# A two-layer hybrid trunk on one core: the logarithm by a polynomial, one more load buffer, and 108 shifted priorities

## The chip, the cores and the metric

The kernel runs on one core of a Trainium2 chip. The metric is the device time of one execution in microseconds; the median of three runs of the kernel before is 618.05 us (617.97 to 618.89). The core's engines work side by side, each through its own queue of instructions: TensorE (PE in the profile, and PEld for its weight loads), VectorE (DVE), ScalarE (ACT), GpSimd (POOL) and SyncE (SP, which here only issues DMAs). They wait for each other at semaphores.

## The reference, cut to what matters

Two layers over 256 tokens of width 1024, in float32. A layer normalises its input, sends it through one combined projection `w_in` (1024 x 9808), runs three causal attention mixers of eight 64-wide heads on parts of the result, gates each, projects each with its `w_branch`, adds the three under per-channel gates, and sends the sum through `w_out` onto the residual. The third mixer adds a running sum of log-sigmoids to its logits, and this is where the logarithm is:

```python
proj = jnp.einsum('bsd,de->bse', rms_norm(x, gain), w_in)
...
# mixer b: the 64 keys with the largest index score, per query
rel = jax.nn.relu(jnp.einsum('bqhd,bsd->bqhs', qi, k_idx))
isc = jnp.einsum('bqh,bqhs->bqs', wi, rel)
ival, idx = lax.top_k(isc, top)
...
# mixer c: forgetting attention
log_f = jax.nn.log_sigmoid(f_logit + f_bias)          # 256 tokens x 8 heads
csum = jnp.cumsum(log_f, axis=1)
s = q @ k.T * scale + (cq[..., :, None] - csum[:, :, None, :])
...
merged = sum(sigmoid(merge_logit) * y for the three branches)
x = x + merged @ w_out
```

## The kernel before

All weights stream once from HBM through a ring of 1 MB buffers, `raw` (three of them, `R_RAW = 3`). To keep float32 accuracy on TensorE each weight is split in two parts, a rounded high part `wh` and the rest `wl`, and each product is three matmuls: high by high, high by low, low by high. ACT writes `wh` (a copy of 128 x 1024, L374), DVE subtracts it from `raw` to give `wl` (L378), and PE reads both. Each has a ring of six buffers.

PE's work comes in *units*. A unit of kind B computes 128 columns of a projection for all 256 tokens: 24 matmuls of 128 x 256 into one PSUM bank `proj`. A unit of kind A has 128 tokens and 512 columns; a unit Y belongs to `w_branch`. Between the units stand the small groups of the attention: the scores of a pair of heads (six matmuls into the banks `s`, of which there are two, L604 and L606), the transposes of the probabilities (three per head into a bank `t`, L692), and the product with the values (eight matmuls into the only bank `o`, L708 to L711).

A layer runs: norm and transpose of the input, the values of mixer a, the small unit `kwf` (index key, index weights, forget logits), four units of the index query `qi` with their scores, then the mixers a, c and b with the units of the merge gates and of `w_branch` between them, then `w_out`. What this text calls the *index stage* is the stretch from `kwf` to the first attention of mixer a, 30 to 90 us in layer 0 and 330 to 390 us in layer 1. There, ACT takes the ReLU of the index scores out of the two `s` banks (L818 and L819), DVE adds them up over heads into `isc` (L827, L829) and then finds the 64 largest of each row in eight rounds of MAX8 and MATCH_REPLACE8 (L849, L850). Rotary embedding goes through DVE and POOL: a shuffle into `rsh` and a product into `rr` on DVE (L468, L470), a product and a sum on POOL (L469, L471). Of `rsh` and `rr` there are two buffers each.

In the index stage also stands the logarithm, in `wf_cols`, on tiles of 128 x 16 called `fz`: with z the logit, e = exp(-|z|) and u = ln(1 + e) on ACT (L777, L778), then nine small DVE instructions (L782 to L790) that correct u for small e and end in min(z, 0) - u. Two matmuls on PE (L796, L797) then make the running sum, `csum`. The function ln is in another activation table than the others, so ACT loads a table ahead of ln and another ahead of the next tanh (L863).

No order is written out by hand. The program records its operations one after the other, each with its engine (or engines), an estimated cost, what it reads and writes, and a *key*, mostly the number of its unit plus an offset. `Plan.run` then lays them out: it takes the engine that can start something earliest, and on it, of the operations that could start by then, the one with the smallest key. The instructions are issued in that order, and each engine's queue keeps it.

```python
lim = best[e] + slack.get(e, 0.0)
t, _, _, o, w = min((c for c in cand if c[4][0] == e and c[0] <= lim), key=lambda c: (c[1], c[2]))
```

Of the kernel before, what the change touches and what calls it, by code (L numbers as in the profile page):

```python
# [9 lines left out]
F32 = mybir.dt.float32  # L10
F32R = mybir.dt.float32r
AF = mybir.ActivationFunctionType
ALU = mybir.AluOpType
# [14 lines left out]
NR = {"a": 0, "b": 1, "c": 2}  # L28

C_ID, C_UT, C_MASK, C_ROPE, C_END = 0, 128, 256, 512, 1024  # L30
SWAP = list(range(8, 16)) + list(range(0, 8)) + list(range(16, 32))

R_RING = 6
R_RAW = 3
TAIL = {"ACT": 95.0, "DVE": 85.0, "POOL": 0.0, "PE": 0.0, "SP": 0.0}
STEP = 24.0
SPLIT_LEAD = 2.0
# [14 lines left out]
def shape_constants():  # L52
    c = np.zeros((128, C_END), np.float32)
    i = np.arange(128)
    c[:, C_ID:C_ID + 128] = np.eye(128)
    c[:, C_UT:C_UT + 128] = i[:, None] <= i[None, :]
    diag = np.where(i[None, :] <= i[:, None], 0.0, MASKED)
    c[:, C_MASK + 128:C_MASK + 256] = diag
    inv = np.power(np.float32(500000.0), -np.arange(0, 16, 2, dtype=np.float32) / np.float32(16))
    ang = np.arange(S, dtype=np.float32)[None, :] * inv.astype(np.float32)[:, None]  # L60
    cos, sin = np.cos(ang).astype(np.float32), np.sin(ang).astype(np.float32)
    ct = np.ones((128, S), np.float32)
    st = np.zeros((128, S), np.float32)
    for b in (0, 64):
        ct[b:b + 8] = cos
        ct[b + 8:b + 16] = cos
        st[b:b + 8] = -sin
        st[b + 8:b + 16] = sin
    c[:, C_ROPE:C_ROPE + 256] = ct
    c[:, C_ROPE + 256:C_ROPE + 512] = st  # L70
    return c


CUR = [""]
# [21 lines left out]
class Plan:  # L96
# [8 lines left out]
    def op(self, ways, reads, writes, key, lag=0.0, name="", touch=()):  # L105
        o = Op()
        o.ways, o.key, o.lag, o.name, o.margin, o.port, o.half = ways, key, lag, name, 0.0, False, False
        deps, o.bufs = {}, []
        for t in reads:
            for d in t.w:  # L110
                deps[id(d)] = d
        for t in writes:
            for d in t.w + t.r:
                deps[id(d)] = d
        for t in reads:
            t.r.append(o)
        for t in writes:
            t.w, t.r = [o], []
        for t in {id(t): t for t in list(reads) + list(writes) + list(touch)}.values():
            if isinstance(t, Buf):  # L120
                if t.no is None:
                    t.no = self.made[t.tag] = self.made.get(t.tag, -1) + 1
                t.left += 1
                o.bufs.append(t)
        o.deps = list(deps.values())
        o.n, o.out, o.need, o.end = len(self.ops), [], 0, None
        for d in o.deps:
            if d is not o:
                d.out.append(o)
                o.need += 1  # L130
        self.ops.append(o)
        return o
# [111 lines left out]
def hybrid_trunk(ctx, tc, x, norm_gain, w_in, forget_bias, w_branch, w_out, final_gain, consts, out):  # L244
# [97 lines left out]
    plan.tag("pth", pts[:1])  # L342
    plan.tag("ptl", pts[1:])
    plan.tag("bd", bd)
    for nm, n, cols, dt in (("rsh", 2, S, F32), ("rr", 2, S, F32),
                            ("th", 2, S, F32), ("g", 4, S, F32), ("e", 4, 384, F32), ("st", 8, 8, F32),
                            ("fb", 2, 384, F32), ("ot", 2, S, F32), ("t8", 4, 8, F32), ("mth", MTH, S, F32)):
        tag(nm, n, [128, cols], dt)
# [409 lines left out]
    def wf_cols(l, key):  # L758
        ps = Buf("t")

        def tr():
            for t in range(2):
                PE.transpose(T(ps)[:, t * 16:t * 16 + 16], wf[64:80, t * 128:(t + 1) * 128], ident[64:80, 64:80])
        pe(tr, 220.0, [k_wf, k_id], [ps], key, "wf")
        v = lambda: T(ps)[:, :32].rearrange("p (t c) -> p t c", t=2)
        sc = float(np.float32(8 ** -0.5 * 64 ** -0.5))
        dve(lambda: DVE.tensor_scalar(widx, v()[:, :, 0:8], sc, None, op0=ALU.mult), 16, [ps], [k_widx], key, "wf")
        z, na, e, u, c, lf = [fz[:, i].rearrange("p (t c) -> p t c", t=2) for i in range(6)]
        fb = fbias[:, l:l + 1, :].to_broadcast([128, 2, 8])

        def pre():
            DVE.tensor_tensor(z, v()[:, :, 8:16], fb, op=ALU.add)
            DVE.scalar_tensor_tensor(na, z, -1.0, z, op0=ALU.mult, op1=ALU.min)
        dve(pre, 0, [ps, k_fb], [k_lf], key, "lf", 300.0)

        def ln():
            ACT.activation(e, na, AF.Exp)  # L777
            ACT.activation(u, e, AF.Ln, bias=1.0)  # L778
        act(ln, 0, False, [], [k_lf], key, "ln", 1540.0)
        act(lambda: None, 0, False, [k_lf], [], key - 1, "table", 1190.0)  # L780

        for f in (lambda: DVE.tensor_scalar(c, e, 1.0, None, op0=ALU.add),  # L782
                  lambda: DVE.tensor_scalar(na, c, 1.0, None, op0=ALU.is_equal),
                  lambda: DVE.tensor_scalar(c, c, -1.0, 5e-8, op0=ALU.add, op1=ALU.max),
                  lambda: DVE.reciprocal(c, c),
                  lambda: DVE.tensor_tensor(c, c, e, op=ALU.mult),
                  lambda: DVE.tensor_tensor(u, u, c, op=ALU.mult),
                  lambda: DVE.tensor_tensor(na, na, e, op=ALU.mult),
                  lambda: DVE.tensor_tensor(u, u, na, op=ALU.add),
                  lambda: DVE.scalar_tensor_tensor(lf, z, 0.0, u, op0=ALU.min, op1=ALU.subtract)):  # L790
            dve(f, 0, [], [k_lf], key + 10, "lf", 100.0, port=True)

        cs = Buf("t")

        def cum():
            PE.matmul(T(cs)[:, :16], ut, lf.rearrange("p t c -> p (t c)"), start=True, stop=False)  # L796
            PE.matmul(T(cs)[:, 8:16], ones, lf[:, 0], start=False, stop=True)  # L797
        pe(cum, 400.0, [k_lf, k_cst], [cs], key + 10, "csum", MARGIN)
        w = lambda: T(cs)[:, :16].rearrange("p (t c) -> p t c", t=2)
        dve(lambda: DVE.tensor_copy(csum, w()), 16, [cs], [k_cs], key, "csum")  # L800
        dve(lambda: DVE.tensor_scalar(ncs, w(), -1.0, None, op0=ALU.mult), 16, [cs], [k_cs], key, "csum")
        rep, k_rep = wf.rearrange("p (t r c) -> p t r c", t=2, r=16), Tok()
        dve(lambda: DVE.tensor_copy(rep, w().unsqueeze(2).to_broadcast([128, 2, 16, 8])), S, [cs], [k_rep, k_wf], key + 10, "csum")
        pt = Buf("t")

        def tr2():
            for t in range(2):
                PE.transpose(T(pt)[:, t * 128:(t + 1) * 128], wf[:, t * 128:(t + 1) * 128], ident)
        pe(tr2, 225.0, [k_rep, k_id], [pt], key + 10, "cT", MARGIN)
        act(lambda: ACT.activation(cT, T(pt)[:, :S], AF.Copy), S, True, [pt], [k_rep, k_cT], key + 10, "cT")  # L810
# [306 lines left out]
```

## Time and profile before

| | |
|---|---|
| runs, median (range) | 618.05 us (617.97 to 618.89) |
| the profiled execution's own time | 618.74 us |
| its span, first to last instruction | 616.9 us |
| PE busy | 606.5 us, 4804 matmuls |
| PEld busy | 581.1 us |
| DVE busy | 534.5 us |
| ACT busy | 451.7 us |
| POOL busy | 95.0 us |
| granted TensorE clock, mean | 0.997 |
| moved by DMA | 107.32 MB, 174 GB/s |

The profile page gives busy times of engines, a chain of work that ended last, and groups of instructions. The trace behind it can be asked for the instructions in order of time and for who waited for whom. Matmuls are pipelined, so two that follow each other overlap in the trace, and "PE busy" is not a measure of PE at its peak; from one start to the next is. A number in brackets at a row's end, such as `[0.37 <-ACT tmp L819]`, is the idle time of the engine just before it and what ended it.

### The profile page before, as it was taken

What the parts mean: (1) busy time and instruction counts of PE and PEld (TensorE: products, weight loads), DVE (VectorE), ACT (ScalarE), POOL (GpSimd) and SP (SyncE); (2) the same over time, 40 slices, a digit from 0 to 9 for tenths busy, and PEclk for the clock granted to TensorE, in tenths of its full rate; (3) what the DMA queues carried; (4) which work ended last, traced back from release to release, by engine and by line L of the source; (5) the groups of instructions that cost most, each with busy time, mean ns of one, the idle gap of its engine ahead of it and who ended that gap; (6) DMA issues with size and microseconds to landing.
All of it is one profiled execution on the core that took longest, in us unless ns stands there. A gap on an engine that the chain in (4) does not pass through costs nothing.

```text
span 616.9 us, 12615 instructions
## 1 busy us (share of the span) xinstructions
PE 606.5 (98%) x4804; PEld 581.1 (94%) x4804; DVE 534.5 (87%) x1322; ACT 451.7 (73%) x948; POOL 95.0 (15%) x101
## 2 busy tenths in 40 slices
PE   8999999999999999999999999999999999999995
PEld 6899999999998999999889999998999989999985
DVE  7899999985998889988588999998678988999773
ACT  5788398876996778775587866997688766987541
POOL 1251242000000233200006305300000013220001
PEclk9999999999999999999999999999999999999998
DMA  8962765655554563575555639455637365453711
GB/s 283 304 195 90 226 171 191 200 171 172 171 173 136 180 197 99 175 237 173 158 170 174 204 114 276 141 170 185 209 103 231 112 201 157 155 169 122 257 35 69
DMA packets 96156, 107.32 MB, mean 174 GB/s; under 512 B 4576, under 2 KB 84832, under 8 KB 96096
## 3 DMA queue, kind: packets, MB, share of 16 engines
q1 hardware_dynamic: 95808, 106.13, 54.7%
q8 instruction: 37, 0.61, 0.4%
q10 hardware_dynamic: 288, 0.39, 0.2%
q14 instruction: 23, 0.19, 0.1%
HBM read 103.37 MB, written 1.05 MB: 169 GB/s over the span
## 4 chain that ended last, share of the span: by engine, by line
PE 78%; DVE 13%; ACT 4%; issue 2%; DMA 1%; POOL 1%; SPq 0%; POOLq 0%; DVEq 0%; ACTq 0%
PE proj L419 68%; DVE wl L378 5%; PE t L692 3%; DVE isc L850 2%; PE proj L996 1%; PE s L604 1%; PE s L606 1%; DVE t L849 1%; DMA x<-in_x_dram 1%; DVE isc L829 1%; DVE rsh L468 1%; ACT wh L374 1%; PE o L708 1%; PE o L711 1%; DVE rr L470 1%
## 5 line engine op out<-in xcount | busy, mean ns | idle before, releaser
L419 PE MATMUL proj<-hTh,wh 128*128 128x256 f32 (+1 forms) x1040 | 270.1, 278 | 0.0
L419 PE MATMUL proj<-hTl,wh 128*128 128x256 f32 (+1 forms) x1040 | 269.7, 277 | 0.0
L378 DVE TENSOR_TENSOR wl<-raw,wh 128x1024 fp32r<-128x1024 f32 (+1 forms) x190 | 235.5, 1248 | 38.3 <-ACT wh L374 37.7
L374 ACT ACTIVATE wh<-raw 128x1024 fp32r<-128x1024 f32 (+1 forms) x190 | 199.0, 1053 | 51.1 <-PE proj L419 41.3
L419 PE MATMUL proj<-hTh,wl 128*128 128x256 f32 (+1 forms) x1040 | 234.0, 278 | 0.0
L419 PEld LDWEIGHTS proj<-hTh,wh 128*128 128x128 f32 (+1 forms) x1040 | 194.7, 187 | 0.2
L419 PEld LDWEIGHTS proj<-hTl,wh 128*128 128x128 f32 (+1 forms) x1040 | 194.6, 187 | 0.3
L419 PEld LDWEIGHTS proj<-hTh,wl 128*128 128x128 f32 (+1 forms) x1040 | 175.6, 187 | 0.0
L469 POOL TENSOR_TENSOR rsh<-rsh,cst 128x256 f32<-128x256 f32 (+1 forms) x42 | 35.6, 849 | 351.9 <-DVE rsh L468 351.7
L471 POOL TENSOR_TENSOR rr<-rr,rsh 128x256 f32<-128x256 f32 (+1 forms) x42 | 51.1, 1220 | 8.2 <-DVE rr L470 5.4
L669 ACT ACTIVATE e<-e,st 128x128 f32<-128x128 f32 x96 | 42.7, 446 | 6.9 <-DVE st L665 6.6
L419 PE MATMUL proj<-wh,v 128*128 128x512 f32 (+1 forms) x144 | 35.5, 368 | 0.0
L419 PE MATMUL proj<-og0l,wh 128*128 128x256 f32 x128 | 33.9, 277 | 0.0
L419 PE MATMUL proj<-og0h,wh 128*128 128x256 f32 x128 | 32.4, 278 | 0.0
L419 PE MATMUL proj<-wh,hTh 128*128 128x512 f32 x80 | 32.4, 405 | 0.0
L419 PE MATMUL proj<-wh,hTl 128*128 128x512 f32 x80 | 31.5, 393 | 0.0
L419 PEld LDWEIGHTS proj<-wh,v 128*128 128x128 f32 x144 | 25.2, 188 | 4.7
L419 PE MATMUL proj<-og0h,wl 128*128 128x256 f32 x128 | 28.6, 277 | 0.0
L697 DVE TENSOR_TENSOR ptl<-t,pth 128x384 fp32r<-128x384 f32 x48 | 24.9, 551 | 0.6 <-ACT pth L695 0.6
L419 PE MATMUL proj<-wl,hTh 128*128 128x512 f32 x80 | 24.9, 392 | 0.0
L419 PEld LDWEIGHTS proj<-og0h,wh 128*128 128x128 f32 x128 | 24.0, 188 | 0.0
L419 PEld LDWEIGHTS proj<-og0l,wh 128*128 128x128 f32 x128 | 24.0, 188 | 0.0
(194 smaller groups left out, 1046.1 us busy)
## 6 DMA issues: line engine op xcount, KB each, us to landing
raw<-in_w_in_dram SPq DMA_DIRECT2D x74, 1024.0 KB, 5.3
raw<-in_w_branch_dram SPq DMA_DIRECT2D x24, 512.0 KB, 3.5
raw<-in_w_out_dram SPq DMA_DIRECT2D x8, 1024.0 KB, 6.9
tmp<-wf SPq DMA_DIRECT2D x16, 128.0 KB, 5.2
raw<-in_w_in_dram SPq DMA_DIRECT2D x3, 512.0 KB, 7.9
x<-in_x_dram SPq DMA_DIRECT2D x4, 256.0 KB, 5.1
raw<-in_w_in_dram SPq DMA_DIRECT2D x2, 320.0 KB, 6.0
out_dram<-tmp SPq DMA_DIRECT2D x2, 320.0 KB, 2.5
```

The costliest lines, as they stand in the source:

```text
L374: ACT.activation(p[0].v, sel(c.v), AF.Copy)
L378: DVE.tensor_tensor(p[1].v, sel(c.v), p[0].v.bitcast(F32), op=ALU.subtract)
L419: PE.matmul(o(), a(), b(), start=first and i == 0, stop=last and i == n - 1)
L468: dve(lambda: DVE.stream_shuffle(T(sh)[:np_], a(), SWAP), S, [ps], [sh], key, "rope")
L469: gps(lambda: POOL.tensor_tensor(T(sh)[:np_], T(sh)[:np_], s[:np_], op=ALU.mult), S, [k_rope], [sh], key, "rope")
L470: dve(lambda: DVE.tensor_tensor(T(r)[:np_], a(), c[:np_], op=ALU.mult), S, [ps, k_rope], [r], key, "rope")
L471: gps(lambda: POOL.tensor_tensor(T(r)[:np_], T(r)[:np_], T(sh)[:np_], op=ALU.add), S, [sh], [r], key, "rope")
L604: PE.matmul(o.rearrange("p (h c) -> p h c", h=2), qh[:, sl], kl[:, :, :n], start=True, stop=False)
L669: act(lambda t=t, a=a, n=n, e=e, st=st: ACT.activation(T(e)[:, a:a + n], T(e)[:, a:a + n], AF.Exp, bias=T(st)[:, t:t + 1], scale=-1.0, acc ...
L692: PE.transpose(T(ps)[:, i * 128:(i + 1) * 128], T(es[h])[:, i * 128:(i + 1) * 128], ident)
L697: dve(lambda h=h, src=src: DVE.tensor_tensor(T(pl)[:, h], src(), T(ph)[:, h].bitcast(F32), op=ALU.subtract), 384, [ps, kp[h][0]], [kp[h][1 ...
L850: dve(lambda o=o, t8=t8: DVE.match_replace(o, T(t8), o, TAKEN), n, [t8], [k_isc[i]], key + r * step, "top8")
```

## The change

Five edits go together.

1. The logarithm. ln(1 + e) is computed as 2 atanh(s) with s = e / (e + 2), as an odd polynomial in s with five coefficients. ACT keeps the exponential and loses the logarithm and the two table loads; DVE has ten small instructions in the place of nine.
2. `R_RAW` goes from 3 to 4: four load buffers.
3. `rsh` and `rr` go from two buffers each to four.
4. A table `SHIFT` adds a number between -10 and +2 to the keys of 108 operations, by their place in the recording (the last one in the table is operation 2954).
5. `dynamic_dma_scratch_size=1024` is given to the program's constructor, which leaves SBUF for the new buffers.

Below the table every line of the file stands 14 to 16 lines further down: L374 becomes L390, L378 becomes L394, L692 becomes L708, and so on.

```diff
+ATANH = (2.0, 0.666663146821, 0.400249102795, 0.279606027472, 0.281783350867)
-R_RAW = 3
+R_RAW = 4
...
+SHIFT = {
+    142: -3, 143: -4, 145: -4, 192: -3, 231: -1, 233: -4, 264: -2, 349: -3, 350: 2, 391: 1, 396: -1, 398: -4,
...
+        o.key += SHIFT.get(o.n, 0.0)
...
-    for nm, n, cols, dt in (("rsh", 2, S, F32), ("rr", 2, S, F32),
+    for nm, n, cols, dt in (("rsh", 4, S, F32), ("rr", 4, S, F32),
...
-        def ln():
-            ACT.activation(e, na, AF.Exp)
-            ACT.activation(u, e, AF.Ln, bias=1.0)
-        act(ln, 0, False, [], [k_lf], key, "ln", 1540.0)
-        act(lambda: None, 0, False, [k_lf], [], key - 1, "table", 1190.0)
-
-        for f in (lambda: DVE.tensor_scalar(c, e, 1.0, None, op0=ALU.add),
-                  lambda: DVE.tensor_scalar(na, c, 1.0, None, op0=ALU.is_equal),
-                  lambda: DVE.tensor_scalar(c, c, -1.0, 5e-8, op0=ALU.add, op1=ALU.max),
-                  lambda: DVE.reciprocal(c, c),
-                  lambda: DVE.tensor_tensor(c, c, e, op=ALU.mult),
-                  lambda: DVE.tensor_tensor(u, u, c, op=ALU.mult),
-                  lambda: DVE.tensor_tensor(na, na, e, op=ALU.mult),
-                  lambda: DVE.tensor_tensor(u, u, na, op=ALU.add),
-                  lambda: DVE.scalar_tensor_tensor(lf, z, 0.0, u, op0=ALU.min, op1=ALU.subtract)):
+        act(lambda: ACT.activation(e, na, AF.Exp), 16, False, [], [k_lf], key, "lf")
+
+        s, s2, q = na, c, u
+        for f in (lambda: DVE.tensor_scalar(s2, e, 2.0, None, op0=ALU.add),
+                  lambda: DVE.reciprocal(s2, s2),
+                  lambda: DVE.tensor_tensor(s, e, s2, op=ALU.mult),
+                  lambda: DVE.tensor_tensor(s2, s, s, op=ALU.mult),
+                  lambda: DVE.tensor_scalar(q, s2, ATANH[4], ATANH[3], op0=ALU.mult, op1=ALU.add),
+                  lambda: DVE.tensor_tensor(q, q, s2, op=ALU.mult),
+                  lambda: DVE.scalar_tensor_tensor(q, q, ATANH[2], s2, op0=ALU.add, op1=ALU.mult),
+                  lambda: DVE.scalar_tensor_tensor(q, q, ATANH[1], s2, op0=ALU.add, op1=ALU.mult),
+                  lambda: DVE.scalar_tensor_tensor(q, q, ATANH[0], s, op0=ALU.add, op1=ALU.mult),
+                  lambda: DVE.scalar_tensor_tensor(lf, z, 0.0, q, op0=ALU.min, op1=ALU.subtract)):
...
-    nc = _bacc.Bacc("TRN2", target_bir_lowering=False, num_devices=1)
+    nc = _bacc.Bacc("TRN2", target_bir_lowering=False, num_devices=1, dynamic_dma_scratch_size=1024)
```

What the five edits do to the order is seen at three places. The number and the shapes of PE's matmuls are the same in both programs. In the rows below, a name is a tile and the number behind it says which buffer.

The first place is ACT's queue in the index stage of layer 0, between the ReLU of the second index pair (`tmp_108<-s`) and that of the third. The `q` names are the three forms of an index query that PE reads. Before:

```order
L819 ACTIVATE tmp_108<-s_163 128x512
L591 ACTIVATE qy_87<-qh_81 64x256
L591 ACTIVATE qx_85<-qh_82 64x256
L591 ACTIVATE qx_85<-qy_88 64x256
L591 ACTIVATE qx_83<-qh_80 64x256
L591 ACTIVATE qy_88<-qh_82 64x256
L591 ACTIVATE qx_83<-qy_86 64x256
L863 ACTIVATE acc<-proj_161 128x256
L374 ACTIVATE wh_67<-raw_120 128x1024
L818 ACTIVATE tmp_108<-s_162 128x256
L591 ACTIVATE qy_86<-qh_80 64x256
L819 ACTIVATE tmp_108<-s_163 128x512
```

And in the changed program:

```order
L833 ACTIVATE tmp_108<-s_168 128x512
L877 ACTIVATE acc<-proj_166 128x256
L390 ACTIVATE wh_67<-raw_118 128x1024
L607 ACTIVATE qx_83<-qh_80 64x256
L607 ACTIVATE qy_88<-qh_82 64x256
L832 ACTIVATE tmp_108<-s_167 128x256
L607 ACTIVATE qx_83<-qy_86 64x256
L833 ACTIVATE tmp_108<-s_168 128x512
```

Of the eight instructions that stood between the first ReLU shown and the next one, four remain; four of the copies have moved ahead of the first ReLU.

The second place is PE's queue in layer 1, where the running sum of the logarithm (`fz`) is multiplied in the middle of a unit. Before:

```order
L419 MATMUL proj_161<-hTl,wh_68 128x256
L796 MATMUL t_164<-fz,cst 128x16
L797 MATMUL t_164<-fz,ones 128x8
L419 MATMUL proj_161<-hTh,wl_75 128x256
L419 MATMUL proj_161<-hTh,wh_68 128x256
```

And in the changed program:

```order
L435 MATMUL proj_166<-hTh,wl_75 128x256 x2
L435 MATMUL proj_166<-hTh,wh_68 128x256
L435 MATMUL proj_166<-hTl,wh_68 128x256
L810 MATMUL t_170<-fz,cst 128x16
L811 MATMUL t_170<-fz,ones 128x8
L435 MATMUL proj_166<-hTh,wl_75 128x256
```

It is the same unit of B; the two products have moved 12 matmuls further back in it. In layer 0 they have moved 36 further back.

The third place is DVE's queue in layer 1 at the first pair of mixer a. `ISA e,st<-s` adds the mask to the scores and takes the row's extreme; the reciprocal and the product on `e` follow after ACT's exponential, and PE waits for them with its transposes. Before:

```order
L378 TENSOR_TENSOR wl_74<-raw_118,wh_67 128x1024
L665 ISA e_131,st_135<-s_162,cst 128x128
...
L665 ISA e_132,st_136<-s_163,cst 128x256
L665 ISA st_136 128x1
L673 RECIPROCAL st_135<-st_135 128x1
L378 TENSOR_TENSOR wl_75<-raw_118,wh_68 128x1024
L673 RECIPROCAL st_136<-st_136 128x1
L853 TENSOR_SCALAR selb<-isc 128x128
L680 TENSOR_SCALAR e_132<-e_132,st_136 128x128
```

And in the changed program:

```order
L394 TENSOR_TENSOR wl_74<-raw_119,wh_67 128x1024
L394 TENSOR_TENSOR wl_75<-raw_119,wh_68 128x1024
L681 ISA e_136,st_140<-s_167,cst 128x128
...
L681 ISA e_137,st_141<-s_168,cst 128x256
L681 ISA st_141 128x1
L689 RECIPROCAL st_140<-st_140 128x1
L426 SCALAR_TENSOR_TENSOR qy_88<-rr_129,qh_82 128x256
L696 TENSOR_SCALAR e_136<-e_136,st_140 128x128
L689 RECIPROCAL st_140<-st_140 128x1
```

The weight split `wl_75` stood between the scores and the products of the pair, and stands ahead of the scores now. On PE the two heads' transposes of this pair stood 12 matmuls apart, the first of them right behind the next pair's scores; now both stand together, six matmuls behind those scores.

More of the change, by code (lines that the diff above doesn't have):

```diff
@@ L71, in shape_constants @@
     return c
+SHIFT = {
[10 rows of a table added]
+}
 CUR = [""]
```

9 rows, old and new, of the table SHIFT are left out of this document.

## The prediction

> **What bounds the kernel now.** I read the engines' busy times first, then who waited on PE and on its weight loads, then PE's own rows at the places named there, then ACT's and DVE's rows ahead of them.
>
> ```profile
> span 616.9 us, 12615 instructions
> ...
> PE 606.5 (98%) x4804; PEld 581.1 (94%) x4804; DVE 534.5 (87%) x1322; ACT 451.7 (73%) x948; POOL 95.0 (15%) x101
> ```
>
> PE is at work nearly all the time, so an edit on another engine pays only where PE waits. These are all the waits of the weight loads, which come to a semaphore ahead of their matmuls:
>
> ```profile
> PEld proj L996 <- ACT hTh L527: 1.5, 1, 1.5
> PEld proj L996 <- issue: 1.1, 1, 1.1
> PEld t L911 <- DVE ones L907: 1.1, 1, 1.1
> PEld s L604 <- ACT tmp L819: 1.0, 3, 0.5
> PEld t L796 <- DVE fz L790: 0.8, 2, 0.6
> PEld t L520 <- ACT tmp L501: 0.6, 2, 0.4
> PEld proj L996 <- DVE wl L988: 0.6, 1, 0.6
> PEld t L692 <- ACT e L677: 0.3, 1, 0.3
> PEld o L708 <- ACT bd0h L744: 0.3, 1, 0.3
> PEld s L604 <- DVE st L665: 0.2, 1, 0.2
> ```
>
> Lines 911, 996 and 520 are the program's start (and the same transposes at the layer's change), which the order leaves as it is. What is left is 1.0 + 0.8 + 0.3 + 0.3 + 0.2 = 2.6 us: three scores of the index stage that wait for ACT's ReLU, two running sums that wait for the logarithm's last DVE instruction, and three groups of mixer a's first pairs. No unit waits for `wl` or `wh` after the start. So the kernel is bound by PE's own pace, and the change can win little over 2.6 us, or lose.
>
> A wait costs PE more than its idle time, since the matmuls behind it start more slowly. From the first row of a score to the unit's next row, undisturbed and then at the three waits:
>
> ```profile
> 44.56 0.28 PE L604 MATMUL s<-bd0l,qh 128*128 128x256 f32 x1
> ...
> 45.38 0.28 PE L419 MATMUL proj<-hTh,wh 128*128 128x256 f32 x1
> ...
> 48.14 0.38 PE L604 MATMUL s<-bd0l,qh 128*128 128x256 f32 x1
> ...
> 49.06 0.50 PE L604 MATMUL s<-bd0l,qh 128*128 128x512 f32 x1 [0.37 <-ACT tmp L819]
> ...
> 49.64 0.28 PE L419 MATMUL proj<-hTh,wh 128*128 128x256 f32 x1
> ...
> 340.62 0.28 PE L604 MATMUL s<-bd1l,qh 128*128 128x256 f32 x1
> ...
> 341.70 0.28 PE L419 MATMUL proj<-hTh,wh 128*128 128x256 f32 x1
> ...
> 345.13 0.28 PE L604 MATMUL s<-bd1l,qh 128*128 128x256 f32 x1
> ...
> 346.45 0.28 PE L419 MATMUL proj<-hTh,wl 128*128 128x256 f32 x1
> ```
>
> The undisturbed group takes 45.38 - 44.56 = 0.82 us; the others take 1.50, 1.08 and 1.32. The excess is 0.68 + 0.26 + 0.50 = 1.44 us, where the list has 1.0.
>
> **The change part by part.**
>
> *The logarithm.* Per layer ACT loses two table loads and one small instruction; its rows here:
>
> ```profile
> 28.54 0.20 ACT L777 ACTIVATE fz<-fz 128x16 f32<-128x16 f32 x1
> 28.75 1.28 ACT L778 ACT_TABLE_LOAD   x1
> 30.05 0.22 ACT L778 ACTIVATE fz<-fz 128x16 f32<-128x16 f32 x1
> ...
> 332.23 0.42 ACT L405 ACTIVATE qh<-rr 128x256 fp32r<-128x256 f32 x1 [1.89 <-POOL rr L471]
> ...
> 341.69 1.28 ACT L863 ACT_TABLE_LOAD   x1
> ...
> 48.43 0.57 ACT L819 ACTIVATE tmp<-s 128x512 f32<-128x512 f32 x1
> ```
>
> A switch costs 30.05 - 28.75 = 1.30 us, so ACT gains 2 x 1.30 + 0.22 = 2.8 us in each index stage. PE sees of it only what stands behind the three ReLUs. In layer 0 both loads lie ahead of the ReLU of 48.43 us, whose lateness is 0.68 us; four copies also moved ahead of the previous ReLU, by the order. I take the 0.68 as gone. In layer 1 the first load is followed by 1.89 us in which ACT waits for POOL's rotary sum, so its 1.3 us end in that idle time, and the second load (341.69) comes after the first of the two waits there. So of layer 1 I take the 0.50 as gone and leave the 0.26: together 1.18 us, between 0 and 1.44.
>
> The Trainium skill (ScalarE: Activation LUTs, What ACT_TABLE_LOAD costs) gives about 1283 ns for the load, which agrees with 1.28 here, and a drain of about 1380 ns on top, which this trace does not show, since the next instruction starts 0.02 us behind the load. By its 2.66 us a switch would reach past the 1.89 us of idle, the 0.26 would go as well, and the forecast below would be 0.3 us lower; I go by the trace.
>
> On DVE one small instruction is added per layer; such a one takes 0.17 us here:
>
> ```profile
> L786 DVE TENSOR_TENSOR fz<-fz x2: 163/170/176, 46.8 to 359.8; 128x16 f32<-128x16 f32 x2
> 361.28 0.16 DVE L790 SCALAR_TENSOR_TENSOR fz<-fz 128x16 f32<-128x16 f32 x1
> 361.50 0.40 PE L796 MATMUL t<-fz,cst 128*128 128x16 f32 x2 [0.41 <-DVE fz L790]
> ...
> 362.58 0.41 DVE L633 SCALAR_TENSOR_TENSOR g<-th,proj 128x256 f32<-128x256 f32 x1
> ...
> 239.99 16.36 PE proj L419 x144
> ```
>
> PE's sum in layer 1 moves back by 12 matmuls, 12 x 16.36/144 = 1.4 us, against one more DVE instruction and, by the order, one gating product (0.41 us) more and the same number of weight splits ahead of it: DVE ends about 0.6 us later, PE comes about 0.8 us later net of the waits it no longer has (1.4 us less the 0.26 to 0.76 gone before). That roughly covers the 0.6 us of this wait or leaves a third of it. In layer 0 PE comes 36 matmuls later and DVE has two more splits in between, which about balance. Of the 0.8 us I take 0.5 as won; the ends are 0.8 won and 0.6 lost (the same wait once more).
>
> *The load buffer.* No PE wait is a wait for weights, so earlier loads win nothing directly. They cost nothing either, unless the first of them collides with the loads of the start: it no longer waits for a free buffer, and can go behind the last small load, at 10.97 + 0.43 = 11.40 us and not at 11.85, so the loss is at most 0.45 us. I take 0, as only loads that go after it share its time.
>
> ```profile
> 10.97 0.43 SPq L917 DMA_DIRECT2D fbias<-in_forget_bias_dram  x1
> 11.85 0.38 SPq L366 DMA_DIRECT2D raw<-in_w_in_dram  x1
> ```
>
> *The rotary buffers.* They let DVE's shuffle run ahead of POOL. POOL is busy 15% and SP's queue only issues; their cover is PE's lead of several units. What they can win is the 0.26 us left in layer 1, and I count nothing. *The smaller scratch*: no row of the profile shows anything that uses it, and I count nothing.
>
> *The table.* It can win the three waits of the attention's first pairs, 0.3 + 0.3 + 0.2 = 0.8 us, and it can make new ones. The pair of layer 1 in the order is the one behind this wait:
>
> ```profile
> 386.57 1.28 DVE L378 TENSOR_TENSOR wl<-raw,wh 128x1024 fp32r<-128x1024 f32 x1
> 387.20 0.77 PE L692 MATMUL t<-cst,e 128*128 128x128 f32 x3
> 389.20 0.49 PE L692 MATMUL t<-cst,e 128*128 128x128 f32 x3
> ```
>
> The split of 1.28 us in the middle of the pair's chain is now ahead of it. That shortens the chain but starts it later, and the second head's transposes come 12 matmuls (1.4 us) sooner behind the first's. I take half of the 0.8 as won, 0.4, and one new wait of the smallest size listed, 0.2, lost; the ends are 0.8 won and 1.4 lost (as much again as the index stage loses today).
>
> *The sum.* -1.18 - 0.5 - 0.4 + 0.2 = -1.9 us. The profiled execution took 618.74 us, 1.84 of it outside the span; it would take 616.8. It stands 0.69 us over the median of 618.05, so the median of the changed kernel comes to 616.1.
>
> **The rivals.**
>
> *Every gap of the index stages closes.* The busy time of the weight loads in 75 us of each (span, PE, PEld, DVE, ACT, POOL):
>
> ```profile
> 30.00:105.00 75.00, 74.45 (x643) 73.36 (x642) 72.72 (x199) 60.03 (x124) 24.67 (x24) 1.00 0.55 169
> 330.00:405.00 75.00, 74.32 (x641) 73.27 (x640) 71.74 (x202) 58.61 (x122) 25.10 (x24) 1.00 0.56 170
> ```
>
> Their gaps are 1.64 + 1.73 = 3.4 us, a bit more than the waits because of the slow starts behind them. If all goes, the median is 618.05 - 3.4 = 614.7. For it: the table could have been made for these very gaps. Against it: the groups of the attention end several of them by their shape alone. The Trainium skill (Perfetto Trace Analysis, Identifying the Most-Contended Engine) says the busy share of the weight loads, not of the matmuls, tells the headroom; by that rule these gaps would be headroom.
>
> *New waits take their place.* The order puts groups just behind the moment at which they are expected to be ready; if that is 0.24 us too early at eight of the groups that moved, the 1.9 us are lost again: 618.0, with 617.4 to 618.6 for six to ten such groups. For it: the 2.6 us of today are such waits. Against: ACT has 2.8 us more room in just these stages.
>
> *Slower: the paired transposes.* In layer 1 all four pairs of mixer a now have both heads' transposes together. DVE is busy 95% or more of this stage (71.74 of 75.00), and with a split ahead of the scores it begins the chain up to 1.3 us later, and PE stands with nothing between. A lateness of 0.8 us at each of the four, 3.2 us, is the point at which the kernel is 0.2% slower (3.2 - 1.9 = 1.3); 1.3 us at each gives 618.05 - 1.9 + 5.2 = 621.4. Against it: PE's scores themselves stand 18 matmuls later there, 2.0 us.
>
> **How the numbers follow.** The forecast has 0.50, the closed gaps 0.15, the replaced waits 0.23, the paired transposes 0.12. By 0.2%, 1.2 us, a measurement of this kernel tells a change from none: under 616.8 is faster, over 619.3 slower. The forecast's own range is 615.3 to 617.0, so nearly all of it is faster: 0.46 + 0.15 = 0.61; same 0.04 + 0.23 = 0.27; slower 0.12. The range of 614.4 to 618.6 takes in the first three cases, down to the closed gaps and 0.3 for the drain, up to the replaced waits and the 0.45 of the loads; it leaves out the slower one.
>
> **What would show it.** Right: five table loads become one; the waits on L833 (the ReLU) and L804 (the last `fz`) go from the weight loads' list or fall under 0.3 us; the weight loads' gaps in the index stages fall from 3.4 to about 1.7 us; the rest of the trace is as before. Wrong: rows such as `PEld t <- DVE e` or `PEld s <- DVE st` of over 0.5 us in the two mixer a stages, a wait for `wl`, or a start that takes longer than before.

## The result, and the profile after

The changed kernel takes 614.67 us (median of four runs, 614.60 to 615.16); the kernel before, on the same chip, 618.03 us. The ratio is 0.9941, interval 0.9925 to 0.9956: 3.4 us faster, where I forecast 1.9. It is the time of the first rival (every gap of the index stages closes, 614.7), though the gaps did not all close, as shown below. The profiled execution took 614.60 us, 1.8 of it outside the span.

The page after, first lines:

```profile
span 612.8 us, 12606 instructions
...
PE 603.8 (99%) x4804; PEld 580.1 (95%) x4804; DVE 535.1 (87%) x1323; ACT 446.5 (73%) x942; POOL 95.4 (16%) x102
```

DVE and POOL have nearly the same work, ACT has 5.2 us less (of five table loads one is left), and PE does the same 4804 matmuls in less time. These are all the waits of the weight loads that are listed (us in total, times, longest):

```profile
PEld proj L1010 <- issue: 1.1, 1, 1.1
PEld proj L1010 <- ACT hTh L543: 1.1, 1, 1.1
PEld t L925 <- DVE ones L921: 1.1, 1, 1.1
PEld t L536 <- ACT tmp L517: 0.8, 2, 0.4
PEld proj L1010 <- DVE wl L1002: 0.6, 1, 0.6
```

Only the lines of the start and of the layer's change are left (1010, 925 and 536 are 996, 911 and 520 of before). The ReLU, the last `fz` and the three groups of mixer a's first pairs are gone, and nothing new stands in their place. The same two windows of 75 us as in the prediction (span, PE, PEld, DVE, ACT, POOL, clock, DMA share, GB/s):

```profile
30.00:105.00 75.00, 75.00 (x658) 74.73 (x657) 73.53 (x202) 60.38 (x124) 23.22 (x24) 1.00 0.58 182
330.00:405.00 75.00, 75.00 (x656) 74.64 (x656) 74.46 (x204) 59.66 (x124) 22.07 (x22) 1.00 0.56 168
```

The weight loads' gaps are 0.27 + 0.36 = 0.63 us; they were 3.37. The difference is 2.74 us. But each window also holds 15 matmuls more than before (658 for 643, 656 for 641), and 30 of them at 75.00/657 = 0.114 us are about 3.4 us: the slow starts behind a wait are counted as busy, so the gaps tell less than what closing them brings. DVE is busier in the window of layer 1 (74.46 for 71.74): its listed waits there come to 3.1 us before and to 1.1 after.

Where the rest lies is seen by comparing the same place in PE's queue in both traces: the nth matmul, counted from 0, at points where the two queues have come back to the same work (start of the matmul, us):

| nth matmul | before | after | won since the row above | what lies between |
|---|---|---|---|---|
| 150 | 29.66 | 29.22 | 0.43 | the start |
| 316 | 49.64 | 48.47 | 0.73 | layer 0, score behind the ReLU |
| 467 | 67.31 | 65.79 | 0.36 | layer 0, running sum |
| 632 | 86.59 | 84.82 | 0.24 | layer 0, scores that waited for `st` |
| 746 | 99.63 | 97.50 | 0.37 | layer 0, first product with the values (`o`) |
| 2550 | 332.52 | 330.28 | 0.10 | the rest of layer 0 |
| 2668 | 347.15 | 344.13 | 0.79 | layer 1, scores behind the ReLU |
| 2836 | 367.10 | 363.42 | 0.65 | layer 1, running sum |
| 3041 | 391.04 | 387.10 | 0.26 | layer 1, transposes of the first pair |
| 4803 | 610.44 | 606.30 | 0.21 | the rest |

Without the start it is 3.71 us: 1.52 at the ReLUs, 1.01 at the running sums, 0.87 at the first pairs, 0.31 scattered. The start is not the change's: over the 16 traces of this study the 150th matmul begins at 28.75 to 29.66 us, at 29.19 in the mean of the eight with four load buffers and at 29.11 in the mean of the eight with three, and the trace of before happens to have the latest. That goes some way to explain why its own time stood 0.69 us over the median. Behind the start a trace can repeat closely: the changed kernel has 577.08 us from the 150th matmul to the last in both of its traces. I use this stretch, called *the middle* below, to tell variants apart; before it is 580.79.

### The profile page after: what moved, and what is told of

Read it like the earlier page. It is cut to its first block, busy times and chain, and to the rows that moved or that the text cites. A ratio compares the mean times of both kernels' runs of the same rounds, so it can differ in the third digit from the quotient of the medians.

```text
span 612.8 us, 12606 instructions
## 1 busy us (share of the span) xinstructions
PE 603.8 (99%) x4804; PEld 580.1 (95%) x4804; DVE 535.1 (87%) x1323; ACT 446.5 (73%) x942; POOL 95.4 (16%) x102
## 4 chain that ended last, share of the span: by engine, by line
PE 96%; DMA 1%; issue 1%; SPq 0%; ACT 0%; DVE 0%; POOL 0%; POOLq 0%; ACTq 0%
PE proj L435 84%; PE t L708 3%; PE s L622 2%; PE s L620 2%; PE proj L1010 1%; DMA x<-in_x_dram 1%; PE o L727 1%; PE o L724 1%; PE o L726 0%; PE o L725 0%; PE t L536 0%; PE s L536 0%; SPq L995 0%; SPq L931 0%; POOL fsum L579 0%
## 5 line engine op out<-in xcount | busy, mean ns | idle before, releaser
L394 DVE TENSOR_TENSOR wl<-raw,wh 128x1024 fp32r<-128x1024 f32 (+1 forms) x190 | 235.0, 1245 | 31.4 <-ACT wh L390 30.6
L390 ACT ACTIVATE wh<-raw 128x1024 fp32r<-128x1024 f32 (+1 forms) x190 | 199.4, 1054 | 49.4 <-PE proj L435 47.2
L485 POOL TENSOR_TENSOR rsh<-rsh,cst 128x256 f32<-128x256 f32 (+1 forms) x42 | 33.8, 807 | 321.6 <-DVE rsh L484 321.3
L487 POOL TENSOR_TENSOR rr<-rr,rsh 128x256 f32<-128x256 f32 (+1 forms) x42 | 52.4, 1250 | 3.0
L685 ACT ACTIVATE e<-e,st 128x128 f32<-128x128 f32 (+1 forms) x96 | 42.7, 448 | 7.5 <-DVE st L681 7.1
```

What stands on the lines that cost most here:

```text
L390: ACT.activation(p[0].v, sel(c.v), AF.Copy)
L394: DVE.tensor_tensor(p[1].v, sel(c.v), p[0].v.bitcast(F32), op=ALU.subtract)
L485: gps(lambda: POOL.tensor_tensor(T(sh)[:np_], T(sh)[:np_], s[:np_], op=ALU.mult), S, [k_rope], [sh], key, "rope")
L487: gps(lambda: POOL.tensor_tensor(T(r)[:np_], T(r)[:np_], T(sh)[:np_], op=ALU.add), S, [sh], [r], key, "rope")
L685: act(lambda t=t, a=a, n=n, e=e, st=st: ACT.activation(T(e)[:, a:a + n], T(e)[:, a:a + n], AF.Exp, bias=T(st)[:, t:t + 1], scale=-1.0, acc ...
```

## The experiments

Each is told with its time, that of the kernel before in the same group (618.4 to 618.6, medians), and its middle.

### The logarithm's work in a fixed order

The first two runs exchange only what the logarithm's instructions do, in slots that the planner places as it did.

```diff
 # the kernel before, order unchanged
             ACT.activation(e, na, AF.Exp)
-            ACT.activation(u, e, AF.Ln, bias=1.0)
...
+        def two():
+            DVE.tensor_scalar(s2, e, 2.0, None, op0=ALU.add)
+            DVE.reciprocal(s2, s2)
+        for f in (two,
+                  lambda: DVE.tensor_tensor(s, e, s2, op=ALU.mult),
...
```

> The order of before is kept on every engine to the instruction; only the logarithm's work is exchanged (the polynomial's ten DVE instructions stand in the nine old slots, ACT loses ln and two table loads per layer). Theory (the time is made of single waits; the logarithm pays for the waits on ReLU alone): the three ReLU waits of before go, 1.50 us by the difference of the two traces (0.70 in layer 0, 0.80 in layer 1); the two waits on the last fz stay and grow by one DVE instruction of 0.17 us each, and the three first-pair waits stay (0.83 us). So 618.03 - 1.50 + 0.3 = 616.8 us, between 616.4 and 617.2. Rival A (the order did all of it, the freed ACT time lies off the path): 618.0 to 618.4. Rival B (the logarithm did all of it): 614.7.

Measured: 615.70 us, ratio 0.9955 (0.9942 to 0.9967), middle 578.18, so 2.61 us won: more than the theory's 1.5, less than everything. By the table's stations the ReLUs gave 0.73 and 0.65, but the running sums gave 0.32 and 0.67 too, though DVE had an instruction more in each, and the `st` scores of layer 0 0.24. Two of mixer a's waits are what is left beside the start:

```profile
PEld t L693 <- ACT e L678: 0.3, 1, 0.3
PEld o L709 <- ACT bd0h L745: 0.2, 1, 0.2
```

Both the theory and its rivals are wrong on the running sum: a wait for DVE went when ACT lost work.

```diff
 # the changed kernel, order unchanged
-        act(lambda: ACT.activation(e, na, AF.Exp), 16, False, [], [k_lf], key, "lf")
+        def ln():
+            ACT.activation(e, na, AF.Exp)
+            ACT.activation(u, e, AF.Ln, bias=1.0)
+        act(ln, 16, False, [], [k_lf], key, "lf")
...
+        for f in (lambda: None,
+                  lambda: DVE.tensor_scalar(c, e, 1.0, None, op0=ALU.add),
...
```

> The order of the changed kernel is kept on every engine to the instruction; the logarithm's work is the old one again (exp, table load, ln, table load on ACT; nine DVE instructions in ten slots). Theory (the new order has PE's scores only 0.5 to 1.4 us behind ACT's ReLUs, so it needs the 2.8 us that ACT was freed of): in layer 0 ACT has no idle time between the loads and the second score, so the three scores that follow (slack 0.93, 0.52, 0.63 us in the changed kernel's trace) wait about 1.8 + 0.4 + 0.3 = 2.4 us; in layer 1 ACT's waits for POOL's rotary sums (0.49 and 0.42 us) and slacks of 0.8 to 2.1 us take most of it, 0 to 0.8. Total 614.67 + 2.4 to 3.2 = 617.1 to 617.9. Rival A (the order alone does it): 614.5 to 615.2, and no weight load waits for L833/L835.

Measured: 616.39 us (ratio 0.9969, 0.9957 to 0.9981), middle 579.07. This is outside the theory's range: the old logarithm costs 1.99 us in the new order, not 2.4 to 3.2. The waits are on the two ReLU lines, as expected, but one of the three is in layer 1, and one on `st` comes with them:

```profile
PEld s L620 <- ACT tmp L835: 0.7, 2, 0.4
PEld s L620 <- ACT tmp L834: 0.4, 1, 0.4
PEld s L620 <- DVE st L681: 0.4, 1, 0.4
```

So the freed ACT time is worth 2.61 us in the old order and 1.99 in the new one, and the new order (with its buffers) 1.72 with the old logarithm and 1.10 with the new. Neither does it alone, and they overlap.

### Is it ACT's time, or DVE's chain?

```diff
             ACT.activation(e, na, AF.Exp)
-            ACT.activation(u, e, AF.Ln, bias=1.0)
+            ACT.activation(u, e, AF.Exp)
```

> Before, with one word changed: ACT computes exp a second time where it computed ln, so the four table loads inside the layers go (two per layer, 1.28 us each) and every other instruction and every queue's order stays. It leaves the logarithm out: the forget gates come out wrong. Theory now (ACT's lateness is the one cause: it delays the ReLUs that PE waits for, and through wh and qh it delays DVE, which has no idle time to make it up, so the last fz comes late too): the waits on L819 and on L790 both go, DVE's waits on ACT's wh and qh in the index stages (1.3 us in each layer) go, the gaps of the weight loads in the two 75 us index windows fall from 3.37 to about 1.25 us, and the time is that of the polynomial in the old order, 615.7, within 615.2 to 616.2. Rival (the running sum waited for DVE's own chain, which the polynomial made shorter or freer, as I assumed in the prediction): only the ReLU waits go, the two fz waits (1.03 us together) stay: 616.6 to 617.0.

Measured: 615.70 us (ratio 0.9952, 0.9940 to 0.9965), middle 578.19: the polynomial's effect to 0.01 us, with DVE's nine instructions as they were. The waits that are left beside the start are the same two:

```profile
PEld t L692 <- ACT e L677: 0.3, 1, 0.3
PEld o L708 <- ACT bd0h L744: 0.2, 1, 0.2
```

So in the old order the polynomial matters only because it frees ACT of the four table loads inside the layers. Of the five in before, the one of the start remains in this run's list:

```profile
L501 ACT ACT_TABLE_LOAD x1 | 1.3, 1283 | 3.5 <-DMA x<-in_x_dram 3.5
```

Why the running sum comes sooner is read from DVE's own waits in the trace of before. In layer 0 from 40 to 62 us, and in layer 1 from 340 to 362.5 us, up to the sums, these are all of them:

```profile
DVE qy L406 <- ACT qh L405: 0.7, 1, 0.7
DVE wl L378 <- ACT wh L374: 0.6, 1, 0.6
...
DVE wl L378 <- ACT wh L374: 1.1, 2, 0.6
DVE qy L406 <- ACT qh L405: 0.2, 1, 0.2
```

In each layer DVE stands 1.3 us for ACT, and is busy for nearly all the rest (20.49 of 22.0 us and 21.12 of 22.5), so it cannot make it up: the last `fz` is late by that. With exp in the place of ln the same stretches show no such wait in layer 0 and one of 0.2 us in layer 1, and PE finds `fz` ready. The last DVE instruction on `fz` and PE's sum, in layer 0 of before and then in both layers of this run:

```profile
60.68 0.16 DVE L790 SCALAR_TENSOR_TENSOR fz<-fz 128x16 f32<-128x16 f32 x1
60.90 0.40 PE L796 MATMUL t<-fz,cst 128*128 128x16 f32 x2
...
58.80 0.15 DVE L790 SCALAR_TENSOR_TENSOR fz<-fz 128x16 f32<-128x16 f32 x1
59.39 0.29 PE L796 MATMUL t<-fz,cst 128*128 128x16 f32 x2
...
358.09 0.16 DVE L790 SCALAR_TENSOR_TENSOR fz<-fz 128x16 f32<-128x16 f32 x1
358.47 0.29 PE L796 MATMUL t<-fz,cst 128*128 128x16 f32 x2
```

With exp, the sum starts 0.44 us behind the end of `fz` in layer 0 and 0.22 in layer 1, with no wait listed; in before it was 0.06 in both (361.28 + 0.16 to 361.50 in layer 1), with a wait.

How much sooner DVE comes is read by counting from a matmul ahead of the stage, the 150th in layer 0 and matmul 2550 in layer 1. The last `fz` ends 31.19 and 28.93 us behind it in before and 29.88 and 27.56 with exp: 1.31 and 1.37 us sooner, which is about what DVE had waited. In layer 1 the new order with the old logarithm (the run above) has 29.68, and the changed kernel 28.48. So the new order alone makes DVE 0.75 us later there, and the freed ACT time brings 1.20 back.

### The table and the buffers

> The changed kernel with an empty table: polynomial, four load buffers, four rotary buffers, small scratch, laid out freely. Theory (only the table moves PE's groups behind the moment their operand is really there; the planner's own costs put them too early): the ReLU waits are gone, a wait on the last fz in one or both layers (0.35 to 0.7 us each) and waits of mixer a's first pairs (0.25 to 0.33 us each) stay: 614.67 + 1.0 to 2.2 = 615.7 to 616.9 us. Rival (polynomial and buffers do it, the table only stirs): 614.4 to 615.0.

(The edit: `SHIFT = {}`.) Measured: 614.91 us (ratio 0.9945, 0.9933 to 0.9958), middle 577.35. The rival was right: without the table the planner's own layout already has no wait but the start's, and the windows show nearly the same as the changed kernel:

```profile
30.00:105.00 75.00, 75.00 (x657) 74.73 (x656) 73.99 (x204) 60.76 (x126) 22.03 (x23) 1.00 0.59 185
330.00:405.00 75.00, 75.00 (x656) 74.48 (x655) 73.83 (x203) 59.24 (x122) 21.09 (x22) 1.00 0.55 166
```

> The changed kernel with an empty table a second time, on the same chip as the changed kernel itself. Theory (the table closes 0.16 us of gaps, 0.79 less 0.63): 0.1 to 0.3 us above the changed kernel. Rival (the difference of 0.24 us was the chip's): within 0.1 us of it.

> The changed kernel itself, for the pairs of this group: 614.7 us, with the scatter of the start. Theory: the start (the moment of the 150th matmul, 29.22 us in the first trace, 28.75 to 29.00 in four others) comes out at 28.7 to 29.3, without relation to the change.

Measured on one chip: 614.96 us without the table, 614.42 with it (0.9942, 0.9930 to 0.9955, and 0.9933, 0.9920 to 0.9945); the intervals overlap. The middles are 577.34 and 577.08, as in the first traces (577.35 and 577.08). By the times the difference is 0.54 us, more than the 0.1 to 0.3 that I expected, but within the scatter; by the middles the 108 shifts are worth 0.26 us here. The starts were 29.46 and 29.37, a little above what I expected for the changed kernel.

```diff
 # before, with the buffers alone
-R_RAW = 3
+R_RAW = 4
...
-(("rsh", 2, S, F32), ("rr", 2, S, F32),
+(("rsh", 4, S, F32), ("rr", 4, S, F32),
...
+dynamic_dma_scratch_size=1024
```

> Before with four load buffers, four rotary buffers and the small scratch alone; the old logarithm, no table. Theory (no weight load waits for weights, so the buffers win nothing themselves; they only make the planner lay things out a little differently): 618.0, between 617.2 and 618.8, with the same kinds of waits (ReLU, fz, first pairs) in other places. Rival (earlier loads shorten the start or close waits): under 617.0. Of the start: theory none, the first matmul group after the 28 opening transposes within 0.3 us of before.

Measured: 616.98 us (ratio 0.9978, 0.9970 to 0.9987), middle 579.35: 1.44 us won with the old logarithm, outside the theory's range and just under the rival's 617.0, though the start (28.96) is like the others'. By the windows the gain is in layer 0, and layer 1 is nearly as before:

```profile
30.00:105.00 75.00, 75.00 (x656) 74.53 (x655) 74.50 (x200) 60.75 (x127) 23.36 (x23) 1.00 0.61 186
330.00:405.00 75.00, 74.25 (x639) 73.10 (x638) 72.34 (x203) 60.98 (x127) 20.95 (x22) 1.00 0.54 167
```

The gaps are 0.47 and 1.90, for 1.64 and 1.73 before. The next runs put the polynomial on and take the buffers singly (each with an empty table unless it says otherwise).

> Before with the polynomial alone, laid out freely by the planner (three load buffers, two rotary ones, empty table). Theory (the polynomial closes what hung on ACT; which of mixer a's first pairs still wait is the luck of the layout): 615.7 as in the old order, within 615.0 to 616.4. Rival (the buffers are needed for the free layout to be as good as without the table it was, 614.9): the same range, but then over 615.5; rival (the polynomial alone gives it all once the layout is free): 614.6 to 615.1.

> Polynomial and the fourth load buffer, no table, two rotary buffers. To keep the start out, I go by the time from PE's 150th matmul to its last, which agreed to 0.01 us between two traces of the same kernel (577.34 and 577.35, 577.08 twice); the polynomial alone has 579.07 there, polynomial with all buffers 577.35. Theory (it is the rotary buffers that count: they let DVE run ahead of POOL's 735 ns steps in the plan, so that the index queries and their scores find other places; the load buffer only lets transfers start earlier, and no matmul waits for a weight): 578.4 to 579.3, time 614.9 to 615.8. Rival (the load buffer): 577.4, time 614.9 or less.

> Polynomial and four rotary buffers, no table, three load buffers. Theory (the rotary buffers count): 577.2 to 577.8 from the 150th matmul to the last, time 614.9. Rival (the load buffer counts): 578.5 or more, time 615.4 or more.

> The changed kernel (polynomial, table, small scratch) with three load buffers and two rotary ones. Theory (the table was fitted to one layout; on another, the same shifts land on groups with other lateness and are worth nothing in particular): within 0.6 us of the polynomial alone, 578.4 to 579.7 from the 150th matmul on. Rival (the shifts put PE's groups later wherever they are): 577.1 to 577.6.

> Before with the table alone (old logarithm, old buffers). Theory (as the run before: a fitted table on another layout): within 0.8 us of before either way, 580.0 to 581.6 from the 150th matmul on. Rival (the table's shifts are what closes the running sum and the first pairs, as I had it in the prediction): 579.0 to 579.6, with no wait on L804 and none of mixer a's.

Measured:

| kernel | median us | ratio (interval) | middle us |
|---|---|---|---|
| polynomial alone | 615.40 | 0.9949 (0.9935 to 0.9963) | 579.07 |
| polynomial, fourth load buffer | 615.31 | 0.9948 (0.9936 to 0.9960) | 578.03 |
| polynomial, rotary buffers | 614.57 | 0.9936 (0.9924 to 0.9949) | 577.39 |
| polynomial, table, old buffers | 614.93 | 0.9942 (0.9929 to 0.9954) | 577.46 |
| table alone, old logarithm and buffers | 618.47 | 0.9996 (0.9987 to 1.0005) | 579.99 |

The polynomial alone came inside the theory's range. Its trace is that of an execution of 616.46 us, the longest of its six; against the median that is 1.06 us too long. If all of that lies behind the start, its usual middle is some 578.0; this is an estimate, as no trace of a usual execution was taken. In that execution PE waited for scores' operands and a running sum:

```profile
PEld s L620 <- DVE st L681: 1.2, 2, 0.9
PEld t L810 <- DVE fz L804: 0.4, 1, 0.4
```

Then the polynomial alone has 578.0 to 578.2 in either layout, the load buffer adds nothing, and the rotary buffers bring it to 577.39, which was the theory for these two (the load buffer's middle lay below the range that I gave; I had set it from the long execution). The table with the old buffers brings it to 577.46: here the theory that a fitted table is worth nothing on another layout is wrong and the rival right. So the table or the rotary buffers each take 0.5 to 0.8 us of what the polynomial leaves, and all of the order and buffers together 0.9 to 1.1. With the old logarithm the table alone leaves 0.8 us of the ReLU's waits and one wait of the running sum, and has more on `st` (0.9 for 0.2):

```profile
PEld s L620 <- DVE st L681: 0.9, 3, 0.5
PEld s L620 <- ACT tmp L835: 0.5, 2, 0.3
PEld t L812 <- DVE fz L806: 0.3, 1, 0.3
PEld s L620 <- ACT tmp L834: 0.3, 1, 0.3
```

Its middle is 0.80 us shorter than before, at the edge of the theory's range, its time the same. In the profiled execution the span ended 7.38 us behind the start of the last matmul, for 6.49 in before. Whether all its executions end so is not known, and why is open.

Do the buffers act, or the other layout that the planner makes with them? In the last two, the tiles are exchanged behind the planner's back, in the order of the first run:

```diff
                     b.slot = f.pop(0)
+                    if b.tag in MORE:
+                        more = MORE[b.tag]
+                        b.slot[1] = more[0]
+                        more.append(more.pop(0))
```

> The polynomial in the old order, as in the first of these runs, and every engine's queue to the instruction the same; only that rsh and rr now go round four tiles in place of two. Theory (the rotary buffers count because the planner, seeing four, lays PE's groups elsewhere; by themselves they relieve nothing that PE waits for): 578.1 to 578.3 from the 150th matmul to the last, as with two (578.18), and the same two waits of mixer a's first pairs. Rival (the buffers themselves let DVE's shuffles run ahead of POOL, so the index queries come earlier): 577.3 to 577.9.

> The polynomial in the old order, every queue the same; only that the weight loads go round four buffers in place of three, so that each can start one buffer earlier. Theory (no matmul after the start waits for a weight): 578.1 to 578.3, and the DMA share of the 14 to 30 us window rises from 0.98 to about 1.09 as in the runs with four load buffers. Rival (earlier weights let ACT and DVE split them earlier and so relieve the first pairs): 577.3 to 577.9.

Measured: 615.63 us (ratio 0.9956, 0.9943 to 0.9968) with four rotary buffers and 615.24 (0.9950, 0.9937 to 0.9964) with four load buffers; middles 578.57 and 578.12, for 578.18. With the load buffer it is the same, and the DMA share from 14 to 30 us is 1.09, as expected. With the rotary ones this execution has one more wait, which the trace with two buffers does not have:

```profile
PEld s L612 <- DVE st L673: 0.5, 1, 0.5
```

It takes the middle 0.39 us above the two-buffer run, out of the range that I gave; the rival's gain is not there. ACT's waits for POOL's sum, from 330 to 405 us, stay: here those of one line with two buffers (first row) and with four, and the other line has 2.6 and 2.5 us:

```profile
ACT qh L406 <- POOL rr L472: 2.2, 2, 2.0
```

```profile
ACT qh L413 <- POOL rr L479: 2.2, 2, 2.0
```

So in the order of before neither kind of buffer relieves anything by itself. What helps is that the planner, seeing four, puts instructions into another order. Whether that other order needs the four buffers was not tried, and which of the moved instructions brings the gain was not singled out.

## Why the prediction was wrong

The measured 614.67 us lies under the 615.3 to 617.0 of the forecast itself. In the middle, which leaves the start out, 3.71 us were won where the terms add up to 1.88. The difference is 0.34 at the ReLUs, 0.51 at the running sums, 0.47 at the first pairs, 0.20 for a new wait that did not come, and 0.31 scattered, whose cause is open.

*What bounds the kernel*: right. Of the 3.71 us, 3.40 lie at the places where PE waited, where the waits went and the slow starts behind them. The Trainium skill (Perfetto Trace Analysis, Identifying the Most-Contended Engine) judges TensorE's headroom by the busy share of the weight loads, beside the share of peak arithmetic, and not by that of the matmuls; the trace agrees in direction: 2.74 us of the weight loads' gaps closed. Here the gaps told too little, as the middle won 3.71.

*The ReLU term*, -1.18: 1.52 measured. The excess of 1.44 that I had worked out was nearly the whole; what failed was leaving the 0.26 of layer 1's first score in. That score is in the 0.79 of the table. For the logarithm alone the reasoning about ACT's idle time nearly held: in the run with exp for ln, where only ACT's loads went, the first group takes 339.73 - 338.78 = 0.95 us for 1.08, the second 343.98 - 343.17 = 0.81 for 1.32, and the stretch gave 0.63. The rest came with the order, which I had not credited here.

*The running sum*, -0.5 of 0.8: 1.01 measured, the first of the two large errors. The step that failed is "DVE ends about 0.6 us later, PE comes about 0.8 us later": I costed DVE's queue by the instructions that the order had added, and put what ACT's freed time does for DVE at nothing. The order alone does make DVE 0.75 us later in layer 1, but in the changed kernel DVE comes 0.45 us sooner than before. It had been late because it stood 1.3 us per layer for ACT's `wh` and `qh`, and I read the waits of PE and the rows of ACT, but not the waits of DVE. The run with exp for ln shows it, with DVE's instructions and the order untouched: 0.99 us come back at the running sums (0.32 and 0.67). Moving the sum back by 36 and 12 matmuls was not needed for it, though in layer 0 it would have been enough: with the old logarithm in the new order the sum starts 0.49 us behind `fz` there, and only 0.06 in layer 1. The 1.01 is also more than the 0.8 of the list, because I had added the slow start behind a wait to the ReLUs alone.

*The first pairs*, -0.4 of 0.8: 0.87 measured, the second. Halving it was a guess between the ends, and the upper end came. It was credited to the table alone; with the polynomial, the planner's free layout with all the buffers and no table does it too, 0.81 us at the same places. One of the three (the `st` scores, 0.24) goes with ACT's loads already.

*One new wait*, +0.2: none came. In other layouts of this study waits on `st` of up to 0.9 us did appear, so such a wait was possible, but this layout has none.

*The rotary buffers, counted at nothing*: right for the buffers as tiles, wrong for the layout. "They let DVE's shuffle run ahead of POOL" is not what helps here; with the order of before fixed they bring nothing, and ACT's waits for POOL stay. I had taken a capacity that the planner reads for one that the hardware uses. The load buffer and the start: right, nothing either way.

*The rivals.* "Every gap closes" was given 0.15, and every wait of the list behind the start went. That its time came to 0.03 us is luck: of its 3.37 us of gaps 2.74 closed, the middle won nearly 1 us more than that, and with other starts the difference of the medians is 3.36 in the first measurement and 4.04 in the second. What is left, 0.63, stands at no listed wait; that some groups end a gap by their shape alone, as I held against this rival, fits it but was not tested. The paired transposes of layer 1 cost nothing: PE is past those of the first pair 0.26 us sooner against the rest, not 0.8 later. The replaced waits did not come either (at 0.24 us each, six to ten of them give 617.6 to 618.5, not the 617.4 to 618.6 that I wrote).

*The table loads.* The Trainium skill (ScalarE: Activation LUTs, What ACT_TABLE_LOAD costs) has 1.28 us for the load and about as much again for a drain. The load agrees (1283 ns in the row above); no row shows the drain, so the 0.3 us that the lower end of my range took for it has no row behind it. Taking two switches, 2.6 us by ACT's rows, out of each layer gave 1.3 us of PE's time per layer (0.73 + 0.32 + 0.26 and 0.63 + 0.67), about half. By an estimate from that page's figures, 5.3 us a layer, it would be a quarter.

## What to carry to other kernels

Where the engine that bounds the kernel waits for an engine that is 95% busy, ask for whom *that* engine waits: an instruction taken from a third engine, here ACT, busy 73% of the span and some 80% of the two windows, can close the wait, and its price is the lateness handed on, not its own length alone. A buffer count or a cost that a planner reads is part of the order; fix the order and change only the work, then fix the work and change only the order, before either gets the credit. Edits that loosen the same stage do not add up: here the table and the rotary buffers each closed more than half of what the polynomial had left. So a wait that several edits can close should not be halved for each: here the sum of halves was too low.

## What the runs showed that I had not expected

In the programs that were traced twice, the noise is nearly all in the first 30 us. From the 150th matmul to the last, the changed kernel has 577.08 us twice, the one without table 577.35 and 577.34, and the two runs that free ACT in the old order 578.18 and 578.19, while the 150th matmul itself comes at 28.75 to 29.66 us. So 0.1 us could be read here from one trace each, where the whole times of five executions left some 0.8 us on either side (0.9942 to 0.9967 of 618). It fails where a wait comes in some executions of a program and not in others. The polynomial alone seems to be such a case: two of its six executions took over 616.2 us, four under 615.6, and the one traced, of 616.46, has 1.2 us of waits on `st`. What makes DVE late there is open.
